# GpSimd makes two of the four weight sums of three feed-forward units

## The chip, the cores and the metric

One core of one Trainium2 chip runs the whole program in one launch. The metric is the device time of that launch in microseconds (us), as the median of several runs. All inputs start in the chip's memory, the output ends there.

## The reference, cut to what matters

Two decoder layers over 512 tokens of width 1024, in float32. The part that the change touches is the feed-forward block of each layer:

```python
h = rms_norm(x, norm_g[i, 2])
f = (jax.nn.silu(h @ w_gate[i]) * (h @ w_up[i])) @ w_down[i]
x = x + rms_norm(f, norm_g[i, 3])
```

`w_gate` and `w_up` are 1024 by 2816, `w_down` is 2816 by 1024. In front of it stand attention and a short convolution (layer 0) or a spatial gating unit (layer 1).

## The kernel before, in words

**Products.** TensorE multiplies in float32r. Each operand is split into a high part (a cast by ScalarE, `whi` or `hThi`, line 135 for weights) and a low part (operand less high part, by VectorE, `wlo` or `hTlo`, line 136), and three products of parts replace one product.

**Units.** The gate and up products of a layer run in 11 units of 256 hidden columns. In a unit the product is a two by two block product: the weights are cut into the first and the second half of the 1024 rows (chunks "a" and "b", each loaded as one `raw` tile of 128 x 2048 by two DMAs of the SyncE queue) and into two blocks of 128 columns; the 512 tokens are cut into the first and the last 256. Seven products p1 to p7 replace eight. p1, p2 and p4 use quarters of the weights as they are. The other four use sums of quarters, which VectorE makes at line 263 (tile `wsum`): s1 = a1 + b1 for p5, s2 = s1 - a0 for p6, s3 = a0 - a1 for p7, s4 = b0 - s2 for p3. Each product is 24 matmuls of line 679 (`product`), and its weights are a piece made by `Unit.piece`: `split` of a quarter or of a sum, that is one ScalarE cast and one VectorE subtraction of 128 x 1024.

**Order.** `order` is a list of pieces; `ahead` makes them some pieces before their product, and `load` starts the next `raw` chunk when fewer than three are still to be read. There are three `raw` buffers, so a chunk's load waits until the last reader of the chunk three before it has ended. `SOON` and, for the first three units, `SOON_EARLY` tell behind which piece a sum is made, ahead of its own product:

```python
        SOON = {2: ["s1"], 4: ["s3", "s2"], 6: ["s4"]}
        SOON_EARLY = {5: ["s2"], 6: ["s3"], 4: ["s4"]}
```

The three first units (`EARLY`) run p1 and p2 of the first 256 tokens while the last tokens are still being normed (`pre_norm`, `Combined.fill`), and then p5, p6, p4, p7, p3 each. The order of the instructions on VectorE, ScalarE and TensorE is made by the framework's scheduler from this program; on GpSimd it is the order of the program (`manual_schedule`).

**What else stands on GpSimd.** In the units it issues the DMAs that add up blocks of `w_down` in memory (line 186, tile `tsum`). Each stands behind a small instruction of one column, `pace` (line 779), which waits for a ScalarE or VectorE result of the unit and so keeps the DMAs in step. `power` (line 344) is another small GpSimd instruction, in the norms.

**Names.** u0 to u3 are the units of a layer in order; s3u1 is the sum s3 of u1. Line 754 (`plus`) adds a product's PSUM bank to a copy, and frees the bank; line 765 multiplies gate and up; lines 432 and 438 make the parts and sums of the tokens.

Of the kernel before, what the change touches and what calls it, by code (L numbers as in the profile page):

```python
# [72 lines left out]
def trunk(  # L73
# [6 lines left out]
    nc = tc.nc  # L80
# [11 lines left out]
    def nm(base):  # L92
        n_made[0] += 1
        return f"{base}_{n_made[0]}"
# [106 lines left out]
    class Unit:  # L201
# [4 lines left out]
        READS = {1: "a", 2: "b", 4: "b", "s1": "ab", "s2": "a", "s3": "a", "s4": "b"}  # L206
        NEEDS = {5: ["s1"], 6: ["s2"], 7: ["s3"], 3: ["s4"], "s2": ["s1"], "s4": ["s2"]}
        SOON = {2: ["s1"], 4: ["s3", "s2"], 6: ["s4"]}
        SOON_EARLY = {5: ["s2"], 6: ["s3"], 4: ["s4"]}

        def __init__(self, layer, c0):
            self.ws = [col_chunk(w[layer], c0, 256) for w in (w_gate, w_up)]
# [6 lines left out]
        def plan_first(self):  # L219
# [3 lines left out]
            self.READS = {k: v for k, v in self.READS.items() if k not in (1, 2)}  # L223
            self.SOON = self.SOON_EARLY

# [22 lines left out]
        def sum(self, s):  # L248
            if s in self.sums:
                return self.sums[s]  # L250
            for before in self.NEEDS.get(s, []):
                self.sum(before)
            t = ap_.tile([P, 2, 4, P], F32, tag="a", name=nm("wsum"))
            if s == "s1":
                x, y, op = self.quarter("a", 1), self.quarter("b", 1), ALU.add
            elif s == "s2":
                x, y, op = self.sums["s1"], self.quarter("a", 0), ALU.subtract
            elif s == "s3":
                x = self.half["a"].tile[:, :, :, 0:P]
                y, op = self.quarter("a", 1), ALU.subtract  # L260
            else:
                x, y, op = self.quarter("b", 0), self.sums["s2"], ALU.subtract
            nc.vector.tensor_tensor(out=t, in0=x, in1=y, op=op)  # L263
            self.sums[s] = t
            return t

# [40 lines left out]
    def load(upto=1000):  # L307

        while n_loaded[0] < min(upto, len(chunks)):
            if sum(c.left > 0 for c in chunks[:n_loaded[0]]) >= 3:  # L310
                return
            c = chunks[n_loaded[0]]
            c.tile = rawp.tile(c.shape, F32, tag="raw", name=nm("raw"),
                               padded_shape=[P, 2048 // math.prod(c.shape[2:])] + c.shape[2:])
            for part, view in c.views:
                if n_loaded[0] >= 2:
                    nc.sync.dma_start(out=c.tile[part], in_=view)
                else:
                    for ks in (slice(0, 2), slice(2, 4)):
                        nc.sync.dma_start(out=c.tile[:, ks, :], in_=view[:, ks, :])  # L320
            n_loaded[0] += 1
# [506 lines left out]
    with tc.manual_schedule(engines={mybir.EngineType.Activation, mybir.EngineType.DVE}):  # L828
# [37 lines left out]
        for i in range(2):  # L866
            nc.vector.tensor_tensor_reduce(
                out=lam_p, in0=lam_in[:, 2 * i, :], in1=lam_in[:, 2 * i + 1, :], scale=1.0, scalar=0.0,
# [22 lines left out]
        for i in range(2):  # L891
            nc.sync.dma_start(
                out=bias[i],
# [135 lines left out]
    for ch in range(4):  # L1029
# [8 lines left out]
        y = tmp()  # L1038
        nc.scalar.mul(out=y, in_=z[:, 2:514], mul=cols[:, 8 + ch:9 + ch])
        for i in (1, 0):  # L1040
# [8 lines left out]
                                op=ALU.subtract)  # L1049
# [144 lines left out]
```

## Time and profile before

| what | value |
|---|---|
| three runs | 1069.45, 1069.95, 1069.6 us; median 1069.6 |
| the profiled execution's own time | 1071.0 us |
| its span | 1069.1 us |
| TensorE (PE) busy | 1034.5 us, 97% of the span |
| VectorE (DVE) busy | 812.6 us, 76% |
| ScalarE (ACT) busy | 552.1 us, 52% |
| GpSimd (POOL) busy | 191.4 us, 18% |

A row of the timeline is: start in us, length in us, engine, line, operation, written tile <- read tiles, shapes, count, and in brackets the engine's idle time just before and what ended it. A row of the windows is: the stretch, its length, then busy time and number of instructions of PE, PEld (weight loads), DVE, ACT and POOL, then the granted clock of TensorE as a share of full speed, the busy share of the DMA engines and what they moved. Layer 0's units begin at about 233 us, layer 1's at about 722 us.

### The profile page before, as it was taken

The numbers are of one execution on the slowest core, as the hardware profiler recorded it, in microseconds if no ns is written. First come the engines' busy times: TensorE is split into PE (matmuls) and PEld (weight loads), VectorE is DVE, ScalarE is ACT, GpSimd is POOL, SyncE is SP. The second block draws the span as 40 slices with busy tenths as digits, with TensorE's granted clock in tenths as the row PEclk, the third lists the DMA queues.
The fourth block names the chain that finished last, engine by engine and source line by source line (L and its number), as shares of the span: only waits on it lengthen the run. The fifth ranks groups of instructions, "written<-read, shape, count | busy, mean of one in ns | idle before, by whom it ended". The sixth has DMA issues, their size and how long they took to land.

```text
span 1069.1 us, 16311 instructions
## 1 busy us (share of the span) xinstructions
PE 1034.5 (97%) x6395; PEld 923.1 (86%) x6395; DVE 812.6 (76%) x1179; ACT 552.1 (52%) x903; POOL 191.4 (18%) x259
## 2 busy tenths in 40 slices
PE   7999999998999999999999999998899999999997
PEld 5777778887899999998888788888899999998885
DVE  4466654489887996899978454679898797799974
ACT  4456453366453553584846433356455454474842
POOL 1012220011233333220000000010334343220000
PEclk7999999999999999999999999999999999999999
DMA  9231304326788798574744522414789799774741
GB/s 324 57 119 40 119 13 169 94 81 190 191 266 220 188 279 229 159 219 144 280 148 153 163 79 79 138 51 147 207 226 273 201 273 240 177 217 148 257 175 40
DMA packets 112526, 181.10 MB, mean 169 GB/s; under 512 B 5009, under 2 KB 77854, under 8 KB 110402
## 3 DMA queue, kind: packets, MB, share of 16 engines
q1 hardware_dynamic: 96578, 133.92, 38.0%
q0 software_dynamic: 15872, 46.14, 18.7%
q8 instruction: 50, 0.82, 0.3%
q14 instruction: 26, 0.21, 0.1%
HBM read 177.94 MB, written 48.24 MB: 212 GB/s over the span
## 4 chain that ended last, share of the span: by engine, by line
PE 72%; DVE 15%; DMA 4%; ACT 3%; issue 3%; POOL 1%; SPq 0%; DVEq 0%; POOLq 0%; ACTq 0%
PE ps L109 41%; PE ps L679 28%; DVE wlo L136 5%; DMA raw<-in_w_up_dram 3%; DVE wsum L263 3%; ACT whi L135 1%; POOL s L344 1%; DVE hTlo L432 1%; DVE h L503 1%; DVE t L754 1%; ACT j L491 1%; DVE x L552 1%; PE ps L952 1%; DMA raw<-in_w_in_even_dram 1%; DVE t L438 1%
## 5 line engine op out<-in xcount | busy, mean ns | idle before, releaser
L679 PE MATMUL ps<-hThi,whi 128*128 128x256 f32 x1232 | 275.1, 285 | 8.2 <-ACT whi L135 4.9
L679 PE MATMUL ps<-hThi,wlo 128*128 128x256 f32 x1232 | 275.0, 284 | 5.1 <-DVE wlo L136 5.1
L679 PE MATMUL ps<-hTlo,whi 128*128 128x256 f32 x1232 | 274.0, 284 | 1.3 <-DVE hTlo L432 1.3
L136 DVE TENSOR_TENSOR wlo<-raw,whi 128x1024 fp32r<-128x1024 f32 (+1 forms) x206 | 239.7, 1185 | 31.7 <-ACT whi L135 30.7
L135 ACT CAST whi<-raw 128x1024 fp32r<-128x1024 f32 (+1 forms) x206 | 203.6, 1018 | 27.3 <-DMA raw<-in_w_up_dram 7.8
L679 PEld LDWEIGHTS ps<-hThi,whi 128*128 128x128 f32 x1232 | 203.6, 192 | 10.6 <-ACT whi L135 5.9
L679 PEld LDWEIGHTS ps<-hThi,wlo 128*128 128x128 f32 x1232 | 204.0, 192 | 6.6 <-DVE wlo L136 6.5
L679 PEld LDWEIGHTS ps<-hTlo,whi 128*128 128x128 f32 x1232 | 203.8, 192 | 1.9 <-DVE hTlo L432 1.9
L135 ACT CAST whi<-wsum 128x1024 fp32r<-128x1024 f32 x88 | 90.1, 1045 | 57.7 <-DVE wsum L263 50.4
L109 PE MATMUL ps<-whi,wlo 128*128 128x512 f32 x308 | 119.9, 389 | 0.0
L109 PE MATMUL ps<-wlo,whi 128*128 128x512 f32 x308 | 119.8, 389 | 0.0
L109 PE MATMUL ps<-whi,whi 128*128 128x512 f32 x308 | 119.5, 390 | 0.2 <-DVE t L719 0.2
L779 POOL TENSOR_SCALAR pace<-t 128x1 f32<-128x1 f32 x96 | 74.2, 773 | 245.9 <-ACT t L764 172.4
L136 DVE TENSOR_TENSOR wlo<-wsum,whi 128x1024 fp32r<-128x1024 f32 x88 | 105.5, 1219 | 15.9 <-ACT whi L135 15.9
L344 POOL TENSOR_TENSOR s<-s,neg_half 128x1 f32<-128x1 f32 (+1 forms) x40 | 25.0, 627 | 486.8 <-DVE s L484 415.2
L754 DVE TENSOR_TENSOR t<-ps,t 128x512 f32<-128x512 f32 x88 | 58.4, 684 | 32.8 <-ACT t L759 17.6
L759 ACT COPY t<-ps 128x512 f32<-128x512 f32 x66 | 38.5, 583 | 86.2 <-PE ps L679 86.2
L109 PE MATMUL ps<-whi,a 128*128 128x512 f32 x256 | 79.9, 391 | 0.0
L186 POOL DMA_DIRECT2D tsum<-in_w_down_dram x72 | 68.4, 953 | 2.1 <-issue 0.8
L109 PEld LDWEIGHTS ps<-whi,whi 128*128 128x128 f32 x308 | 57.8, 188 | 12.6 <-issue 0.8
L109 PEld LDWEIGHTS ps<-wlo,whi 128*128 128x128 f32 x308 | 57.8, 188 | 11.9
L109 PEld LDWEIGHTS ps<-whi,wlo 128*128 128x128 f32 x308 | 57.8, 188 | 11.9
(143 smaller groups left out, 1485.8 us busy)
## 6 DMA issues: line engine op xcount, KB each, us to landing
tsum<-in_w_down_dram POOLq DMA_DIRECT2D x60, 512.0 KB, 7.0
raw<-in_w_gate_dram SPq DMA_DIRECT2D x44, 512.0 KB, 5.8
raw<-in_w_up_dram SPq DMA_DIRECT2D x44, 512.0 KB, 7.4
raw<-tsum SPq DMA_DIRECT2D x16, 1024.0 KB, 5.0
raw<-in_w_down_dram SPq DMA_DIRECT2D x12, 1024.0 KB, 5.9
raw<-in_w_in_even_dram SPq DMA_DIRECT2D x10, 1024.0 KB, 6.7
tsum<-tsum POOLq DMA_DIRECT2D x20, 512.0 KB, 5.9
raw<-in_w_in_odd_dram SPq DMA_DIRECT2D x8, 1024.0 KB, 5.4
```

Of the source, the lines that this page charges most:

```text
L109: nc.tensor.matmul(out, lhsT, rhs, start=start, stop=stop, **kw)
L135: nc.scalar.copy(out=hi, in_=src)
L136: nc.vector.tensor_tensor(out=lo, in0=src, in1=hi.bitcast(F32), op=ALU.subtract)
L186: return [lambda to=to, of=of, g=g, op=op: nc.gpsimd.dma_start(out=to[:, g, :], in_=of[:, g, :], accum_op=op) for g in self.PAIRS for op, ...
L263: nc.vector.tensor_tensor(out=t, in0=x, in1=y, op=op)
L344: nc.gpsimd.tensor_tensor(out=y0[:, :n], in0=a, in1=neg_half[:, :n], op=ALU.pow)
L432: nc.vector.tensor_tensor(out=self.part(1, p, t), in0=src, in1=self.part(0, p, t).bitcast(F32), op=ALU.subtract)
L438: minus = lambda out, x, y: nc.vector.tensor_tensor(out=out, in0=x, in1=y, op=ALU.subtract)
L679: nc.tensor.matmul(bank[:, m * 256:(m + 1) * 256], piece[a][:, m, k, :], hT.at(b, p)[:, k, :], start=first and m == 0 and i == 0, stop=i = ...
L754: nc.vector.tensor_tensor(out=c, in0=x, in1=y, op=ALU.add)
L759: nc.scalar.copy(out=c, in_=x)
L779: nc.gpsimd.tensor_scalar(out=pace, in0=at[:, 0:1], scalar1=1.0, scalar2=None, op0=ALU.mult)
```

## The change

GpSimd makes s3 and s4 of u0, u1 and u2, in both layers: 12 sums. In those units s3 is now made behind p5's piece, ahead of s2, and s4 behind p6's piece. All other units are as they were.

```diff
-        SOON_EARLY = {5: ["s2"], 6: ["s3"], 4: ["s4"]}
+        SOON_EARLY = {5: ["s3", "s2"], 6: ["s4"]}
...
-            nc.vector.tensor_tensor(out=t, in0=x, in1=y, op=op)
+            helper = self.SOON is self.SOON_EARLY and s in ("s3", "s4")
+            engine = nc.gpsimd if helper else nc.vector
+            engine.tensor_tensor(out=t, in0=x, in1=y, op=op)
```

Lines behind it move down by two. On GpSimd, at the start of layer 0's units, before (`raw_2205` and `raw_2255` are chunks a and b of u0, `raw_2331` is a of u1):

```order
L344 TENSOR_TENSOR s_2241<-s_2239,neg_half 128x1
L779 TENSOR_SCALAR pace_2198<-t_2468 128x1
L779 TENSOR_SCALAR pace_2198<-t_2509 128x1
L186 DMA tsum_77<-in_w_down_dram 128x2x512
L779 TENSOR_SCALAR pace_2198<-t_2575 128x1
```

and now:

```order
L346 TENSOR_TENSOR s_2241<-s_2239,neg_half 128x1
L265 TENSOR_TENSOR wsum_2376<-raw_2205 128x1024
L265 TENSOR_TENSOR wsum_2437<-raw_2255,wsum_2378 128x1024
L781 TENSOR_SCALAR pace_2198<-t_2470 128x1
L781 TENSOR_SCALAR pace_2198<-t_2509 128x1
L186 DMA tsum_77<-in_w_down_dram 128x2x512
L265 TENSOR_TENSOR wsum_2583<-raw_2331 128x1024
L781 TENSOR_SCALAR pace_2198<-t_2575 128x1
```

s3u0 and s4u0 stand ahead of all the paced DMAs, s3u1 behind the second `pace` and its DMA.

On VectorE, at the turn from u2 to u3, before (`raw_2662` and `raw_2798` are a and b of u3, whose sums stay on VectorE; the two instructions of line 754 free the banks of u2's last products):

```order
L136 TENSOR_TENSOR wlo_2967<-raw_2798,whi_2966 128x1024
L263 TENSOR_TENSOR wsum_2970<-raw_2662,raw_2798 128x1024
L136 TENSOR_TENSOR wlo_3007<-raw_2798,whi_3006 128x1024
L754 TENSOR_TENSOR t_2998<-ps_2875,t_2996 128x512
L754 TENSOR_TENSOR t_3002<-ps_2874,t_2996 128x512
L765 TENSOR_TENSOR a_2649<-t_2998 128x256
L263 TENSOR_TENSOR wsum_3010<-raw_2662 128x1024
```

and now:

```order
L136 TENSOR_TENSOR wlo_2967<-raw_2768,whi_2966 128x1024
L265 TENSOR_TENSOR wsum_2970<-raw_2662,raw_2768 128x1024
L136 TENSOR_TENSOR wlo_3007<-raw_2768,whi_3006 128x1024
L265 TENSOR_TENSOR wsum_3010<-raw_2662 128x1024
L265 TENSOR_TENSOR wsum_3012<-wsum_2970,raw_2662 128x1024
L756 TENSOR_TENSOR t_2998<-ps_2875,t_2996 128x512
L756 TENSOR_TENSOR t_3002<-ps_2874,t_2996 128x512
```

Two sums of u3 have come ahead of the two instructions that free the banks. The orders of TensorE and of the SyncE queue are almost as before.

## Rows read from the trace of the kernel before

**Rows 1.** Windows, columns as told above: layer 0's units and the slow clock.

```profile
250.00:265.00 15.00, 12.43 (x98) 11.62 (x97) 15.00 (x21) 8.00 (x12) 2.34 (x1) 1.00 0.48 144
...
304.00:308.00 4.00, 2.21 (x13) 2.01 (x12) 4.00 (x7) 0.84 (x2) 0.91 (x2) 0.83 0.36 137
308.00:312.00 4.00, 4.00 (x28) 4.00 (x27) 2.20 (x4) 1.12 (x2) 0.66 (x1) 0.75 0.66 172
312.00:316.00 4.00, 4.00 (x36) 4.00 (x35) 4.00 (x5) 3.67 (x5) 2.64 (x4) 1.00 0.98 275
```

**Rows 2.** Timeline of PE, layer 0: matmuls that waited.

```profile
256.51 0.38 PE L679 MATMUL ps<-hThi,whi 128*128 128x256 f32 x1 [1.83 <-ACT whi L135]
...
267.23 0.38 PE L679 MATMUL ps<-hThi,wlo 128*128 128x256 f32 x1 [0.88 <-DVE wlo L136]
...
271.84 0.39 PE L679 MATMUL ps<-hThi,wlo 128*128 128x256 f32 x1 [0.88 <-DVE wlo L136]
...
287.39 0.38 PE L679 MATMUL ps<-hThi,wlo 128*128 128x256 f32 x1 [0.88 <-DVE wlo L136]
...
306.46 0.47 PE L679 MATMUL ps<-hThi,whi 128*128 128x256 f32 x1 [1.79 <-DVE t L754]
```

**Rows 3.** Timeline of PE, layer 1: matmuls that waited.

```profile
749.98 0.74 PE L679 MATMUL ps<-hTlo,whi 128*128 128x256 f32 x4 [0.81 <-DVE hTlo L432]
...
761.33 0.74 PE L679 MATMUL ps<-hThi,wlo 128*128 128x256 f32 x4 [0.52 <-DVE wlo L136]
...
777.35 0.74 PE L679 MATMUL ps<-hThi,wlo 128*128 128x256 f32 x4 [0.52 <-DVE wlo L136]
...
795.22 0.74 PE L679 MATMUL ps<-hThi,whi 128*128 128x256 f32 x4 [0.57 <-DVE t L754]
```

**Rows 4.** Timeline of DVE, layer 0: the queue around the sums.

```profile
246.22 0.68 DVE L432 TENSOR_TENSOR hTlo<-t,hThi 128x512 fp32r<-128x512 f32 x1
...
254.17 1.22 DVE L263 TENSOR_TENSOR wsum<-wsum,raw 128x1024 f32<-128x1024 f32 x1
...
257.98 1.22 DVE L263 TENSOR_TENSOR wsum<-raw 128x1024 f32<-128x1024 f32 x1
...
262.05 1.22 DVE L263 TENSOR_TENSOR wsum<-raw,wsum 128x1024 f32<-128x1024 f32 x1
...
268.22 1.22 DVE L263 TENSOR_TENSOR wsum<-raw,raw 128x1024 f32<-128x1024 f32 x1
...
305.13 1.28 DVE L754 TENSOR_TENSOR t<-ps,t 128x512 f32<-128x512 f32 x2
```

**Rows 5.** Chain that ended last: start us, us, what; loads of u2's b and u3's b.

```profile
276.83 6.82 DMA raw<-in_w_up_dram
...
292.38 8.17 DMA raw<-in_w_up_dram
```

**Rows 6.** Timeline of POOL: instructions beside VectorE's, and the second pace.

```profile
96.54 0.93 POOL L933 TENSOR_SCALAR t<-t,s 128x256 f32<-128x256 f32 x1
...
261.02 2.34 POOL L779 TENSOR_SCALAR pace<-t 128x1 f32<-128x1 f32 x1 [19.16 <-ACT t L759]
265.73 0.38 POOL L779 TENSOR_SCALAR pace<-t 128x1 f32<-128x1 f32 x1 [2.37 <-ACT t L764]
...
619.48 1.10 POOL L1115 TENSOR_SCALAR_AFFINE_SELECT a<-a 128x1024 f32<-128x1024 f32 x1
```

**Rows 7.** Timeline of DVE at two of these places.

```profile
96.67 1.43 DVE L136 TENSOR_TENSOR wlo<-raw,whi 128x1024 fp32r<-128x1024 f32 x1
...
619.55 1.04 DVE L350 TENSOR_TENSOR s<-s 128x1 f32<-128x1 f32 x1 [0.66 <-POOL s L344]
```

**Rows 8.** Groups of instructions by line and form: names, count | busy us, mean ns.

```profile
L136 DVE TENSOR_TENSOR wlo<-raw,whi 128x1024 fp32r<-128x1024 f32 x192 | 230.6, 1221 | 31.7 <-ACT whi L135 30.7 <-PE ps L109 0.3
...
L350 DVE TENSOR_TENSOR s<-s 128x1 f32<-128x1 f32 x36 | 6.6, 183 | 11.9 <-POOL s L344 11.2
...
L933 POOL TENSOR_SCALAR t<-t,s 128x512 f32<-128x512 f32 x4 | 6.3, 1566 | 20.1 <-PE ps L918 6.3 <-ACT t L1033 4.9 <-DVE t L1036 4.9
...
L933 POOL TENSOR_SCALAR t<-t,s 128x128 f32<-128x128 f32 x4 | 2.4, 609 | 37.3 <-DVE s L932 33.1 <-ACT a L1010 4.2
```

## The prediction, made before the changed kernel was run

> **What bounds the kernel now.** I read the windows first, to find where TensorE is not full. In layer 0's units, from 250 to 265 us, TensorE is busy 12.43 of 15 us while VectorE is busy all 15 [rows 1]. So VectorE is the bound of that stretch. The PE timeline then says what each stop waits for: a high or low part of a weight sum in u0 and u1 (1.83, 0.88 and 0.88 us), the low part of s1u2 (0.88), and at 306.46 a bank that VectorE frees late (1.79) [rows 2]. Behind that last stop the granted clock falls to 0.83 and 0.75, and 28 matmuls run in 4 us where 36 run afterwards [rows 1]: 8 x 4/36 = 0.9 us lost there and some 0.6 us ahead of it, 1.5 us in all. Layer 1 has the same stops, smaller at the end (0.81, 0.52, 0.52, 0.57) [rows 3]. Once the units run steadily TensorE does not stop, so what the starts gain or lose passes to the end. Nearly all that can be won is in these stops.
>
> **How VectorE and GpSimd meet.** Most of VectorE's instructions here read two tensors from SBUF (wlo, the sums, hTlo<-t,hThi); those with a PSUM operand read one. The trace shows the two engines holding each other up. The one-column `pace` at 261.02 took 2.34 us, the next one 0.38 [rows 6]: it ended only when a row of VectorE instructions with two SBUF operands ended. The other way round: at 619.48 GpSimd begins an instruction that reads 1024 elements and takes 1.10 us, and a one-column VectorE instruction with two SBUF operands, begun 0.07 us later, takes 1.04 us, to the very end of it [rows 6, 7], against a mean of 0.18 [rows 8]. With a GpSimd instruction of 256 elements (96.54, 0.93 us) a wlo begun 0.13 us later took 1.43 us instead of 1.22 [rows 6 to 8]: held by 0.2 us, not to the end. So GpSimd's reading holds VectorE's two-operand instructions, and the hold goes with what is read.
>
> **The change part by part.**
>
> *Price of one sum on GpSimd.* No GpSimd tensor_tensor of this size is in the trace. The hold, T, lies between 1.0 us (the 619.48 row, if both operands were read at once) and the whole instruction at line 933's pace: (1566 - 609)/384 = 2.5 ns an element [rows 8], 0.61 + 896 x 2.5 ns = 2.85 us. I take 2.1 us, twice 1.04, since two operands of 1024 are read and the 619.48 row is the nearest in size.
>
> The Trainium skill (SBUF — State Buffer, Who interferes with whom) has the shared port pair held for the whole instruction, and the loser fully blocked. The 96.67 row does not bear this out: by it wlo would have ended at 97.47 + 1.22 and not at 98.10. The Trainium skill (GPSIMD Engine Reference, Performance versus the Vector engine) gives 4497 ns for a float32 tensor_tensor of 2048 elements; half of it, my estimate, is 2.25 us, and with T at that the sum below would be some 0.6 us longer in each layer.
>
> *Saved on VectorE.* Each sum's slot is 1.13 us, from its start to the next start (257.98, 262.05) [rows 4]. So a sum on GpSimd costs VectorE 2.1 - 1.13 = 1 us, unless it falls beside instructions with a PSUM operand or an idle VectorE.
>
> *Layer 0, u0.* s3u0 needs only chunk a, which is there at about 246.3, and stands first in GpSimd's queue. VectorE runs hTlo until 246.90 [rows 4]; GpSimd gets in at its end and holds to 249.0, where the next instruction would have begun at 246.83: +2.15. Nothing has been saved yet, so s1 and s2, and TensorE's stops for p5 and p6, are later by that. s4u0 needs s2 (254.17 + 2.15, 1.22 long), and gets in behind the instruction then running: +2.1. Only then come the two empty slots: -2.27. s1u1 (268.22) is later by 2.15 + 2.1 - 2.27 = 2.0. The wait for wlo of s3u0 at 267.23 vanishes in TensorE's own lateness.
>
> *u1.* s3u1 stands behind the second `pace` (265.73) [rows 6] and its DMA, whose instruction takes about 0.8 us; with +2.0 it asks at about 268.9, and holds wlo of s4u0 or s1u1: +2.1. The low part for p5u1 (271.84) comes 4.1 us later, and TensorE with it. s4u1 stands behind s2u1, beside two instructions of line 754 with PSUM operands, 1.2 of its 2.1 us covered: +0.9. The two slots give -2.27, and about 1.1 us in which VectorE stood idle in u1 are used up. s1u2 is +4.1 + 0.9 - 2.27 - 1.1 = 1.6 later; s3u2 in front of it adds 2.1: 3.7. TensorE's wait of 0.88 at 287.39 shrinks a little: +3.7 there.
>
> *Loads.* Chunk b of u2 now needs no s3 on VectorE, which released its buffer at about 276.4 (its DMA runs from 276.83) [rows 5]; but s2u1, now 4.1 later, ends at about 277, so this load gains nothing. The same holds for u3's b (292.38, 8.17 us): its release moves by +0.3.
>
> *u2 to u3.* VectorE frees the banks (305.13, two of line 754) behind two more sums than before, 2.27 us: they end at 306.41 + 0.3 + 2.27 = 309.0. TensorE is there at 304.67 + 3.7, less 0.5 for four matmuls that now follow: 307.9. It waits 1.1 instead of 1.79 us and goes on 2.5 later. If the clock holds, 1.5 us come back: +1.0 for layer 0. I take that it holds: the stops of 0.88 us cost no clock, nor did that of 1.83 (granted clock 1.00 in 250 to 265).
>
> *Layer 1.* The same queue, +4.1 at 761.33; s1u2's waits shrink by about 0.4, the stop of 0.57 at 795.22 goes, no clock to win: +3.2.
>
> *At nothing.* The paced DMAs issue up to 3 us later; their sums are read in the down product, over 100 us on. GpSimd's 12 sums are some 30 us of an engine that is 18% busy.
>
> The sum: +1.0 + 3.2 = +4.2 us. The profiled execution took 1071.0 us (span 1069.1, 1.9 around it), 1.4 over the median; against it the sum is 1075.2, and from the median, which the runs are compared by, 1069.6 + 4.2 = **1073.8 us**. About 0.2%, 2.1 us, can be told from no change.
>
> **The rivals.**
>
> *VectorE keeps its turn (faster).* GpSimd may get in only where VectorE reads PSUM or idles; the `pace` at 261.02 passed two ends of VectorE instructions before it got in, which speaks for it; other `pace` rows got in at the first end. Then s3u0 costs 2.1 - 0.6 = 1.5, s4u0 lies beside three PSUM instructions (263.19 to 264.99): 0.3; less 2.27, s1u1 is 0.5 earlier; s3u1 in VectorE's idle 1.1 us behind s1u1 adds 1.0: +0.5. The stop at 287.39 goes (-0.88), that at 306.46 shrinks and the clock holds: -2.5 in layer 0, -1.2 in layer 1. 1065.9 us. It decides where a sum's uncovered hold falls under 1.13 us.
>
> *No hold at all for a two-operand read (faster).* Then VectorE gains 2.27 us before s1u1, s3 ends early, the loads of b come some 5 us earlier, and the stops at 287.39 and 306.46 go with the slow clock: 2.27 + 0.88 + 1.79 + 1.5 = 6.4 in layer 0, 2.27 + 1.1 + 0.57 = 3.9 in layer 1: 1059.3 us. The rows at 96.67 and 619.55 speak against it.
>
> *The hold is the whole instruction at line 933's pace.* T = 2.85, three holds in a row on the path of each layer: 0.75 x 3 x 2 = 4.5 more: 1078.3 us.
>
> **How the numbers follow.** The forecast 0.5 (its own range 1070 to 1077.5), VectorE keeping its turn 0.2, no hold 0.15, the long hold 0.15. The range 1064 to 1079 leaves out the case of no hold and the ends of the others, 0.2 in all. Faster by over 0.2% (under 1067.5): 0.15 + 0.14 + 0.02 = 0.31. Within it: 0.06 + 0.13 = 0.19. Slower: 0.35 + 0.15 = 0.50.
>
> **What would show it.** Right: GpSimd sums of some 2 us or more; at the end of each, a VectorE instruction with two SBUF operands that began early and lasted up to 2 us too long; p5u0's low part some 2 us later, p5u1's 4; no clock below 1.00 around 306; TensorE's stop there near 1 us. Wrong: VectorE instructions of normal length beside the sums; GpSimd sums of 4 us and more that stretch until VectorE reads PSUM (the first rival); loads of u2's b issued several us earlier than 276.4, with p5u2 not later than 287.4.

## The result and the profile after

The changed kernel takes 1084.2 us in the median (1083.3 to 1087.0) beside 1069.8 of the kernel before: a ratio of 1.0135, 95% interval 1.0118 to 1.0153, so 14.5 us slower. The sign was forecast, at half a chance; the size was not: 1073.8 us, with a range that ended at 1079. Two executions of the kernel `fill` (1696 and 3588 us) and one of `s2_then_s3` (1135 us) fell in a slow state of the chip and stand in no figure below.

The page of the changed kernel, busy time by engine (the table of before has 1034.5, 812.6, 552.1 and 191.4 us):

```profile
PE 1038.2 (96%) x6395; PEld 926.8 (86%) x6395; DVE 822.8 (76%) x1167; ACT 551.3 (51%) x903; POOL 227.8 (21%) x271
```

VectorE has lost twelve sums of 1.22 us, 14.6 us of work, and is busy 10 us longer than before: the time in which it is held counts as busy. Groups of the changed kernel by line and form (names, count | busy us, mean ns), the two forms of sum on GpSimd and VectorE's `wlo` of sums:

```profile
L265 POOL TENSOR_TENSOR wsum<-raw 128x1024 f32<-128x1024 f32 x6 | 16.5, 2758 | 4.5 <-DMA raw<-in_w_up_dram 4.5
L265 POOL TENSOR_TENSOR wsum<-raw,wsum 128x1024 f32<-128x1024 f32 x6 | 15.0, 2496 | 35.7 <-DVE wsum L265 27.1 <-issue 8.6
...
L136 DVE TENSOR_TENSOR wlo<-wsum,whi 128x1024 fp32r<-128x1024 f32 x88 | 121.5, 1399 | 17.6 <-ACT whi L135 17.6
```

Before, these 88 `wlo` took 105.5 us, 1219 ns each; they alone have grown by 16 us.

Where it happens is seen by laying two timelines side by side. Timeline of GpSimd after, layer 0: s3u0, s4u0, s3u1 with the DMA ahead of it, s4u1, and s3u2 with its DMA:

```profile
245.35 3.51 POOL L265 TENSOR_TENSOR wsum<-raw 128x1024 f32<-128x1024 f32 x1 [4.15 <-DMA raw<-in_w_up_dram]
256.49 2.67 POOL L265 TENSOR_TENSOR wsum<-raw,wsum 128x1024 f32<-128x1024 f32 x1 [7.63 <-DVE wsum L265]
...
269.55 0.80 POOL L186 DMA_DIRECT2D tsum<-in_w_down_dram  x1
270.37 2.44 POOL L265 TENSOR_TENSOR wsum<-raw 128x1024 f32<-128x1024 f32 x1
...
278.59 2.38 POOL L265 TENSOR_TENSOR wsum<-raw,wsum 128x1024 f32<-128x1024 f32 x1 [3.92 <-DVE wsum L265]
...
286.33 1.24 POOL L186 DMA_DIRECT2D tsum<-in_w_down_dram  x1
287.12 2.91 POOL L265 TENSOR_TENSOR wsum<-raw 128x1024 f32<-128x1024 f32 x1
```

Timeline of VectorE after, the instructions beside them:

```profile
245.56 0.68 DVE L434 TENSOR_TENSOR hTlo<-t,hThi 128x512 fp32r<-128x512 f32 x1
246.16 0.42 DVE L767 TENSOR_TENSOR a<-t 128x256 f32<-128x256 f32 x1
246.50 0.68 DVE L440 TENSOR_TENSOR t<-ps,a 128x512 f32<-128x512 f32 x1
247.10 2.85 DVE L136 TENSOR_TENSOR wlo<-raw,whi 128x1024 fp32r<-128x1024 f32 x1
...
256.87 2.57 DVE L767 TENSOR_TENSOR a<-t 128x256 f32<-128x256 f32 x1
...
268.99 0.42 DVE L767 TENSOR_TENSOR a<-t 128x256 f32<-128x256 f32 x1 [2.47 <-ACT t L766]
269.33 4.56 DVE L136 TENSOR_TENSOR wlo<-wsum,whi 128x1024 fp32r<-128x1024 f32 x2
273.82 1.21 DVE L265 TENSOR_TENSOR wsum<-raw,raw 128x1024 f32<-128x1024 f32 x1
276.14 1.23 DVE L136 TENSOR_TENSOR wlo<-wsum,whi 128x1024 fp32r<-128x1024 f32 x1 [1.11 <-ACT whi L135]
...
278.42 1.28 DVE L756 TENSOR_TENSOR t<-ps,t 128x512 f32<-128x512 f32 x2
279.61 2.44 DVE L136 TENSOR_TENSOR wlo<-wsum,whi 128x1024 fp32r<-128x1024 f32 x1
...
286.71 5.54 DVE L136 TENSOR_TENSOR wlo<-wsum,whi 128x1024 fp32r<-128x1024 f32 x2 [0.52 <-ACT whi L135]
```

Read them in pairs. s4u0 ends at 256.49 + 2.67 = 259.16; the product `a` begun at 256.87 ends at 259.44, 2.15 us longer than its usual 0.42. s4u1 ends at 280.97; the `wlo` begun at 279.61 ends at 282.05, 1.08 us behind it, as if it had only begun there. At 247.10 too `wlo` ends 1.09 us behind the end of s3u0 (248.86). So a VectorE instruction with two SBUF operands makes no progress until GpSimd's sum has ended. Those that read PSUM are untouched: `t<-ps,a` at 246.50 lasts 0.68, as the same instruction did before (at 247.16), and the two of line 756 at 278.42 take 1.28, as they do alone [rows 4].

When a sum gets in differs. s4u0 and s3u1 did so at the first end of a VectorE instruction. s3u0 did not: it was issued at 245.35, passed the ends of `hTlo` and `a`, and ended 2.36 us behind 246.50, where VectorE turned to PSUM; undisturbed a sum takes 2.35 us (s3u0 of layer 1, at 740.04).

And TensorE. Timeline of PE after, layer 0:

```profile
254.01 0.39 PE L681 MATMUL ps<-hThi,whi 128*128 128x256 f32 x1 [0.71 <-ACT whi L135]
255.27 0.39 PE L681 MATMUL ps<-hThi,wlo 128*128 128x256 f32 x1 [0.87 <-DVE wlo L136]
257.48 0.39 PE L681 MATMUL ps<-hThi,whi 128*128 128x256 f32 x1 [1.83 <-ACT whi L135]
260.11 0.58 PE L681 MATMUL ps<-hTlo,whi 128*128 128x256 f32 x1 [2.24 <-DVE hTlo L434]
...
276.16 0.38 PE L681 MATMUL ps<-hThi,whi 128*128 128x256 f32 x1 [2.44 <-ACT whi L135]
277.42 0.38 PE L681 MATMUL ps<-hThi,wlo 128*128 128x256 f32 x1 [0.88 <-DVE wlo L136]
...
295.78 0.38 PE L681 MATMUL ps<-hThi,wlo 128*128 128x256 f32 x1 [0.88 <-DVE wlo L136]
...
313.57 0.39 PE L681 MATMUL ps<-hThi,whi 128*128 128x256 f32 x1 [0.80 <-DVE t L756]
```

Windows after, columns as in rows 1:

```profile
254.00:258.00 4.00, 1.16 (x3) 0.56 (x3) 4.00 (x5) 2.41 (x4) 1.51 (x1) 1.00 0.22 55
258.00:262.00 4.00, 1.90 (x9) 1.90 (x10) 4.00 (x5) 1.53 (x4) 1.16 (x1) 0.54 0.74 248
262.00:266.00 4.00, 4.00 (x24) 4.00 (x23) 4.00 (x7) 2.49 (x4) 0.61 (x1) 0.61 0.23 65
...
278.00:282.00 4.00, 4.00 (x24) 4.00 (x23) 4.00 (x5) 2.61 (x4) 3.41 (x2) 0.60 0.58 161
...
744.00:752.00 8.00, 8.00 (x60) 8.00 (x59) 8.00 (x13) 3.52 (x6) 0.00 (x0) 0.85 0.42 133
...
756.00:760.00 4.00, 3.10 (x14) 3.10 (x15) 4.00 (x6) 1.52 (x4) 0.19 (x1) 0.58 0.48 163
```

The four stops up to 260.11 add to 5.65 us; TensorE worked 1.16 us of the 4 from 254 on, and then ran at the lower of its two levels (1.2 GHz) for most of 258 to 266. A second fall follows the stops of 2.44 and 0.88 us at p5u1. Layer 1 has two falls as well, but the first stands behind a stop of 3.64 us for `h` at 743.44 (1.55 before) and the second behind p6u0's stops; behind p5u1's stops of 2.47 and 0.52 us its clock stays at 1.00. In 4 us TensorE does 36 of these matmuls at full clock [rows 1], so the windows at 258, 262 and 278 lost 0.9 + 1.3 + 1.3 us, those of layer 1 1.3 + 1.5 us.

How late TensorE is at each point, against the kernel before, is worked out from the same matmul in both profiles. The change entered layer 0's units 0.67 us earlier (a matmul at 252.97 before is at 252.30) and layer 1's 6.13 us later (723.65 and 729.78); that is taken off.

| TensorE later by (us) | forecast | layer 0 | layer 1 |
|---|---|---|---|
| p5u0, low part; in layer 1 the stop for `h` ahead of u0 | 2.15 | 255.27 - 254.30 + 0.67 = 1.6 | 743.44 - 735.22 - 6.13 = 2.1 |
| p5u1, low part | 4.1 | 277.42 - 271.84 + 0.67 = 6.3 | 772.35 - 761.33 - 6.13 = 4.9 |
| p5u2, low part | 3.7 | 295.78 - 287.39 + 0.67 = 9.1 | 790.01 - 777.35 - 6.13 = 6.5 |
| bank at the turn to u3 | 2.5 | 313.57 - 306.46 + 0.67 = 7.8 | 807.76 - 795.22 - 6.13 = 6.4 |
| behind the turn | +1.0 and +3.2 | 6.8 | 6.9 |

The sum of the last line, 13.7, less the 0.67, is the 13.2 us between the two profiled spans (1082.3 and 1069.1), to 0.2 us. Between the two layers nothing is added: TensorE is 6.8 us late at 318 us and at 723 us.

### The profile page after: what moved, and what is told of

It reads as the page before. It is cut to its first block, busy times and chain, and to the rows that moved or that the text cites. A ratio compares the mean times of both kernels' runs of the same rounds, so it can differ in the third digit from the quotient of the medians.

```text
span 1082.3 us, 16319 instructions
## 1 busy us (share of the span) xinstructions
PE 1038.2 (96%) x6395; PEld 926.8 (86%) x6395; DVE 822.8 (76%) x1167; ACT 551.3 (51%) x903; POOL 227.8 (21%) x271
## 4 chain that ended last, share of the span: by engine, by line
PE 72%; DVE 17%; ACT 4%; issue 3%; DMA 2%; POOL 1%; SPq 0%; DVEq 0%; POOLq 0%; ACTq 0%
PE ps L109 39%; PE ps L681 29%; DVE wlo L136 6%; DVE wsum L265 3%; DMA raw<-in_w_up_dram 1%; POOL s L346 1%; ACT whi L135 1%; DVE t L756 1%; DVE h L505 1%; ACT j L493 1%; DVE hTlo L434 1%; DVE a L767 1%; DVE x L554 1%; PE ps L954 1%; DMA raw<-in_w_in_even_dram 1%
## 5 line engine op out<-in xcount | busy, mean ns | idle before, releaser
L136 DVE TENSOR_TENSOR wlo<-wsum,whi 128x1024 fp32r<-128x1024 f32 x88 | 121.5, 1399 | 17.6 <-ACT whi L135 17.6
L781 POOL TENSOR_SCALAR pace<-t 128x1 f32<-128x1 f32 x96 | 80.5, 839 | 171.9 <-ACT t L766 140.6
L766 ACT ACTIVATE t<-t 128x256 f32<-128x256 f32 x88 | 36.3, 417 | 62.7 <-DVE t L756 62.6
```

Source lines behind the costliest of these rows:

```text
L136: nc.vector.tensor_tensor(out=lo, in0=src, in1=hi.bitcast(F32), op=ALU.subtract)
L766: nc.scalar.activation(out=c[:, 0:256], in_=c[:, 0:256], func=AF.Silu)
L781: nc.gpsimd.tensor_scalar(out=pace, in0=at[:, 0:1], scalar1=1.0, scalar2=None, op0=ALU.mult)
```

## The experiments

Ratios are those to the kernel before on the same chip, with their 95% intervals; times are medians.

**The order or GpSimd.** The first two kernels part the change in its two halves.

```diff
-            helper = self.SOON is self.SOON_EARLY and s in ("s3", "s4")
+            helper = False
```

> The new order of the sums, with all of them on VectorE. Theory of the hold (the loss comes from GpSimd's sums, each of which stops VectorE's two-operand instructions for about 2.2 us in place of a slot of 1.13): this kernel loses nothing of the 14.6 us; 1068 to 1071 us (s2u0 and with it p6u0 1.1 later, but u2's chunk b loaded 1 to 2 us earlier, so that the stop of 0.88 before p5u2 shrinks). Rival, the order (s2 behind s3, and two more sums of u3 ahead of the instructions that free the banks): at least half of the loss, 1077 us or more.

Measured: 1068.2 us, 0.9987 (0.9975 to 0.9999). The order alone loses nothing and may even gain 0.1%.

```diff
-        SOON_EARLY = {5: ["s3", "s2"], 6: ["s4"]}
+        SOON_EARLY = {5: ["s2"], 6: ["s3"], 4: ["s4"]}
```

(in the changed kernel, the sums still on GpSimd)

> The old order of the sums, with s3 and s4 of u0 to u2 on GpSimd. Theory of the hold: nearly all of the loss, 1081 to 1087 us, since the sums still come in at the same data. Rival, the order: 1070 to 1074 us.

Measured: 1081.6 us, 1.0101 (1.0074 to 1.0128). GpSimd's sums cost most of the loss in either order. Timeline of PE with the new order and all sums on VectorE, and two windows of it:

```profile
258.29 0.38 PE L681 MATMUL ps<-hThi,whi 128*128 128x256 f32 x1 [2.96 <-ACT whi L135]
...
288.93 0.39 PE L681 MATMUL ps<-hThi,wlo 128*128 128x256 f32 x1 [0.54 <-DVE wlo L136]
```

```profile
258.00:262.00 4.00, 3.63 (x19) 3.43 (x20) 4.00 (x6) 2.55 (x5) 0.00 (x0) 0.69 0.79 266
262.00:266.00 4.00, 4.00 (x32) 4.00 (x32) 4.00 (x7) 2.29 (x5) 1.21 (x1) 0.88 0.37 112
```

s2u0 is 1.13 later, as expected, and makes the stop for p6u0 2.96 instead of 1.83; in return the stop of 0.88 before p5u2 is down to 0.54, and the stop of 1.79 at the turn to u3 [rows 2] is gone (its window, 304 to 308, has 35 matmuls at a granted clock of 1.00 where rows 1 have 13 at 0.83). The clock falls here too, behind the one stop of 2.96, but at little price: counted as in the table above (this kernel entered the units 0.64 us later), TensorE is 2.0 us late there (260.45 before, 263.10 here) and 0.7 us at p5u1 (270.58 and 271.89).

**Which sums.** The changed kernel with GpSimd making the sums of fewer units (`number` is the unit's place in its layer), or s4 alone:

```diff
-            helper = self.SOON is self.SOON_EARLY and s in ("s3", "s4")
+            helper = self.number == 0 and s in ("s3", "s4")
```

> New order; GpSimd makes s3 and s4 of u0 alone. Theory of the hold with the clock: VectorE's queue is full there, so both holds pass to TensorE (1.6 and 1.8 us), TensorE's clock falls behind these stops and costs some 2 us more, and some of it is taken up by the stops that follow: +3 to +4 us in each layer, 1076 us (1074 to 1079). Rival, only the holds count and the clock is an onlooker: 2.2 + 2.2 - 2.3 = 2 us in each layer, 1074 us or less. Rival, the sums of u1 and u2 are the loss: 1071 us or less.

Measured: 1073.7 us, 1.0031 (1.0020 to 1.0043): just under the range that the first theory gave, just inside that of its rival without the clock; it does not part them.

```diff
+            helper = self.number in (1, 2) and s in ("s3", "s4")
```

> New order; GpSimd makes s3 and s4 of u1 and u2, those of u0 stay on VectorE. Theory of the hold: s3u1 (2.2 us) and s3u2 (3.2 us with the paced DMA) stand ahead of the first sums of u1 and u2 and pass to TensorE; s4 lies half beside instructions that read PSUM and costs what its slot saves; 2 to 2.5 us come back at the turn to u3 in layer 0: 1075 us (1073 to 1078), and with u0_only it adds up to the change's 14.6 us within 2. Rival, u0's late TensorE is what makes the later sums costly (VectorE idle behind it): u12_only within 2 us of before, 1068 to 1072.

Measured: 1078.0 us, 1.0071 (1.0047 to 1.0095). u1 and u2 are costly with u0 untouched, so the rival that puts it on u0 falls.

```diff
+            helper = self.SOON is self.SOON_EARLY and s == "s4"
```

> New order; GpSimd makes s4 of u0 to u2 alone, s3 is VectorE's. Theory of the hold by place: s4u0 falls among instructions with two SBUF operands (2.2 us, less the slot of 1.13, and the clock), s4u1 and s4u2 lie half beside instructions that read PSUM and cost about what their slot saves: 1069.5 to 1072.5 us, so that s3 makes up most of the loss. Rival, every sum on GpSimd costs the same: half of the 16 us between order_only and the change, 1075 to 1077.

Measured: 1075.3 us, 1.0054 (1.0038 to 1.0070). Missed: the expectation took s4u0 at too little. The time is even in the range of its rival, that every sum costs the same; the next kernel parts the two. Timeline of PE with s4 alone on GpSimd:

```profile
257.02 0.39 PE L681 MATMUL ps<-hThi,whi 128*128 128x256 f32 x1 [2.96 <-ACT whi L135]
259.64 0.58 PE L681 MATMUL ps<-hTlo,whi 128*128 128x256 f32 x1 [2.23 <-DVE hTlo L434]
```

Two stops of 2.96 and 2.23 us, 2.6 us apart: s4u0 brings the second, and the clock is 0.50 from 258 to 262.

```diff
+            helper = self.number in (1, 2) and s == "s4"
```

> New order; GpSimd makes s4 of u1 and u2 alone (four sums), where two instructions that read PSUM stand behind s2 on VectorE. Theory of the hold by place: 1.2 of the 2.2 us of hold are covered, the slot saves 1.13: within 1 us of order_only, 1067.5 to 1069.5 us. Rival, every sum on GpSimd costs the same: 16 us/12 each, 1073 to 1074 us.

Measured: 1070.0 us, 1.0007 (0.9996 to 1.0019), 0.5 us over its range and far from the rival. In its timeline s4u1 (274.65, 2.40 us) lies beside the two PSUM instructions, and the `wlo` behind them takes 2.51: held for 1.3 us, beside a saved slot of 1.13.

Against the order alone (0.9987) the ratios rise by 0.44% for all of u0, 0.84% for u1 and u2, 1.48% for the whole: 4.7, 9.0 and 15.8 us, nearly additive. s4 of u1 and u2 is 0.20%, 2.1 us for four sums; s4u0 is 0.54 - 0.07 = 0.47%, 5.0 us for two; so s3u0 has no price beside the order alone (4.7 - 5.0), and s3 of u1 and u2 has 9.0 - 2.1 = 6.9 us for four. The differences are good to some 2 us each, so that the parts show where the price is high, not how high to a microsecond.

**What is held, and for how long.** In the kernel with u1 and u2 alone, GpSimd's instruction reads one operand:

```diff
+            if helper:
+                nc.gpsimd.tensor_scalar(out=t, in0=x, scalar1=1.0, scalar2=None, op0=ALU.mult)
```

> As u12_only, but GpSimd's eight instructions read one operand (a copy with a scale of 1; the other operand of s3 and s4 of u1 and u2 is left out, so the sums are not made). Theory, the hold goes with what GpSimd reads (0.85 to 1.1 us for 1024 elements, as at 96.67 and 619.48 in the trace of before): VectorE's instructions beside them are 1 us too long instead of 2.2, 1070 to 1073 us. Rival, GpSimd holds VectorE for the whole instruction whatever it reads: at line 933's pace 2.5 to 2.85 us each, 1077 us or more.

Measured: 1072.3 us, 1.0025 (1.0012 to 1.0038), where the two-operand form had 1078.0. Timeline of GpSimd, then of VectorE, in this kernel:

```profile
265.54 2.83 POOL L266 TENSOR_SCALAR wsum<-raw 128x1024 f32<-128x1024 f32 x1
...
269.64 2.79 POOL L266 TENSOR_SCALAR wsum<-raw 128x1024 f32<-128x1024 f32 x1
```

```profile
264.49 3.19 DVE L136 TENSOR_TENSOR wlo<-wsum,whi 128x1024 fp32r<-128x1024 f32 x2
...
269.93 1.85 DVE L136 TENSOR_TENSOR wlo<-wsum,whi 128x1024 fp32r<-128x1024 f32 x1 [1.11 <-ACT whi L135]
```

GpSimd's instruction is longer than a sum, and yet the two `wlo` at 264.49 are 3.19 - 2.35 = 0.84 us too long, and the one at 269.93 ends at 271.78 while GpSimd works until 272.43. (The kernel leaves out an operand, so its result is not the program's.) One operand of 1024 elements holds VectorE for 0.84 us of 2.83; two hold it to the end, 2.2 us.

**The price of the clock.** The changed kernel with matmuls that TensorE does where it stood still. The first try put 20 into a free bank:

> The changed kernel with 20 further matmuls in u0 of each layer (into a bank that is still free, their result is overwritten), placed where TensorE would stop for p6u0 and for the low parts of the tokens. Theory: TensorE's clock falls there because TensorE stood idle, and costs about 2.2 us in layer 0 (258 to 266 us at 0.54 and 0.61) and 1.4 us in layer 1: with the stops filled the clock stays at 1.00 and 2 to 4 us come back, 1080 to 1082.5 us. Rival, the slow clock hides behind VectorE's lateness anyway: 1084 us or, by the added matmuls, up to 1087.

Measured: 1083.5 and 1084.5 us. No trace of these two executions shows whether the matmuls fell into the stops and the clock held, so it decides nothing. The second:

```diff
+                if m == 0 and i == (1 if by_k else 7):
+                    for _ in range(fill):
+                        nc.tensor.matmul(bank[:, 0:256], zeros, hT.at(0, 1)[:, 0, :],
+                                         start=False, stop=False, skip_group_check=True)
...
-                run(q, u, 5)
+                run(q, u, 5, fill=(32, 18)[layer] if i == 0 else 0)
```

> The changed kernel with matmuls of zero weights (32 in layer 0, 18 in layer 1; they add nothing to p5's bank) between the first matmuls of p5u0 and those that wait for the low parts of the tokens, so that TensorE is busy from 255.4 to about 259.7 us instead of standing for 4 us. Theory: the clock fell behind these stops (0.54 and 0.61 from 258 to 266 us) and costs time of its own, because p6u0's end releases the ScalarE copy, the silu and the product a for which VectorE waited 2.5 us at 268.99: 258 to 266 us at 0.9 or more, p5u1 2 us earlier, 1080 to 1082 us in all. Rival: the end is set by VectorE's holds, and the slow clock lies beside them: 1083 to 1085 us at whatever clock.

Measured: 1082.9 us, 1.0130 (1.0113 to 1.0146). That lies just above the theory's range and just under its rival's, and 0.05% under the change's ratio; the time alone does not part them. Windows of this kernel:

```profile
254.00:258.00 4.00, 2.42 (x18) 2.02 (x17) 4.00 (x6) 2.13 (x4) 0.15 (x1) 1.00 0.49 172
258.00:262.00 4.00, 3.25 (x28) 3.05 (x27) 4.00 (x4) 2.72 (x4) 2.59 (x1) 1.00 0.74 234
262.00:266.00 4.00, 4.00 (x36) 4.00 (x35) 4.00 (x6) 2.06 (x3) 0.61 (x1) 1.00 0.10 33
...
768.00:772.00 4.00, 3.77 (x18) 3.47 (x19) 4.00 (x5) 2.06 (x5) 1.56 (x1) 0.57 0.39 111
```

In the first three the clock stays at 1.00, and the wait of 2.47 us at 268.99 on VectorE is gone (`a` follows at 267.87 without a gap). Timeline of PE:

```profile
275.03 0.39 PE L683 MATMUL ps<-hThi,whi 128*128 128x256 f32 x1 [1.97 <-ACT whi L135]
```

This kernel entered the units 0.70 us later than the one before, so p5u1's first matmul (270.58 there) is 3.75 us late here, and in the change 276.16 - 270.58 + 0.67 = 6.25: the first fall of the clock costs 2.5 us in layer 0, and the same 2.5 us are still there behind the turn to u3 (6.8 and 4.3 us late at 318). In layer 1 the clock stays at 1.00 from 752 to 760 too, but only 0.4 us come back (6.5 us late behind the turn, not 6.9). Two things differ there: VectorE waits only 0.57 us for ScalarE behind p6u0 in the change (at 763.89), so there is less to win, and in this kernel the clock falls behind p5u1 (0.57 from 768 to 772), where the change had 1.00. Since the two medians came from different chips, the change and this kernel were then run on one:

> The changed kernel itself, as the yardstick for fill2_again and fill3 on the same chip: 1084 us (1083 to 1086), 1.35% over the kernel before.

> fill2 once more, beside the change on the same chip. Theory, the slow clock behind u0's stops has a price: 1.5 to 3 us under change_again. Rival, the clock only fills time in which TensorE would wait for VectorE: within 0.7 us of it.

Measured: 1086.1 us, 1.0154 (1.0133 to 1.0176), and 1082.4 us, 1.0121 (1.0103 to 1.0140): 3.7 us apart, somewhat more than expected, on intervals that overlap a little. The two profiled executions differ by more (spans of 1086.6 and 1078.3 us), and 3.6 us of that arise between 321 and 686 us, away from the units' starts; at p5u1 it is 6.3 and 3.75 us again, and behind the turn 6.8 and 4.25, so 2.5 us in layer 0 is the better figure. A third kernel added 20 matmuls ahead of p5u1:

> fill2 with 20 more matmuls of zero weights ahead of p5u1, where TensorE stops for 2.4 us in both layers and the clock then falls to 0.60 (278 to 282 us). Theory: the clock stays at 1.00 there too and another 1 to 1.5 us a layer come back: 3 to 6 us under change_again, 1078.5 to 1081 us. Rival: VectorE sets p5u2, so nothing more comes back: within 0.7 us of fill2_again, or above it by the added matmuls.

Measured: 1087.7 us, 1.0169 (1.0148 to 1.0190). It tells nothing of the clock: the added matmuls moved `wlo` and `a` on VectorE in u1 and u2, and two stops of 1.58 and 1.83 us stand at 297.60 and 299.94 that the change does not have; the stop that they were to fill stayed, at 3.10 us. What the second fall costs in layer 0 was not settled. For layer 1 the change's own two executions give a figure. Windows of the first, then of the second, behind p5u1's stops (2.47 and 0.52 us, 2.45 and 0.28 us):

```profile
772.00:776.00 4.00, 3.65 (x30) 3.65 (x31) 4.00 (x5) 2.54 (x4) 2.42 (x2) 1.00 0.32 77
```

```profile
772.00:776.00 4.00, 1.27 (x6) 0.96 (x6) 2.89 (x4) 1.53 (x2) 0.98 (x2) 0.85 0.49 131
776.00:780.00 4.00, 4.00 (x26) 4.00 (x27) 4.00 (x4) 2.62 (x4) 3.05 (x2) 0.73 0.44 127
```

From p5u1 to p5u2 TensorE takes 17.66 us in the first (772.35 to 790.01) and 18.00 in the second (775.73 to 793.73): the fall costs 0.3 us, and VectorE waits 0.26 us for TensorE in between (at 782.50), in the first not at all. So nearly the same stops came with a fall in one execution and without in the other.

**A better order.** Two more orders with all sums on VectorE:

```diff
-        SOON_EARLY = {5: ["s2"], 6: ["s3"], 4: ["s4"]}
+        SOON_EARLY = {5: ["s2", "s3"], 6: ["s4"]}
```

> All sums on VectorE, with s3 of the early units right behind s2 (not ahead of it) and s4 behind p6's piece. If order_only gains because s3 ends earlier and frees its chunk (u2's b loaded earlier, the bank at the turn to u3 not late), and loses 1.1 us at p6 of u0 because s2 waits for s3, then this keeps the gain without the loss: 1066 to 1068 us, TensorE's stop for p6u0 back at 1.8 us from 2.96. If the gain of order_only came from somewhere else, 1068.5 us or more.

Measured: 1073.7 us, 1.0034 (1.0021 to 1.0046). Missed on the wrong side. Its timeline of PE:

```profile
276.31 0.39 PE L679 MATMUL ps<-hThi,wlo 128*128 128x256 f32 x1 [0.86 <-DVE wlo L136]
...
294.06 0.39 PE L679 MATMUL ps<-hThi,wlo 128*128 128x256 f32 x1 [0.88 <-DVE wlo L136]
```

With s3 right behind s2, the `wlo` of s2 comes a slot later while its `whi` does not, and TensorE stops for p6's low part in u1 and u2, where the kernel before has no stop.

```diff
+            self.SOON = self.SOON_EARLY if self.number == 0 else self.SOON_NEXT
...
+        SOON_NEXT = {5: ["s3", "s2"], 6: ["s4"]}
```

> All sums on VectorE; u0 in the old order (s2 at once, since TensorE waits for it there), u1 and u2 in the new one (s3 ahead of s2, so that their chunks are freed early). Theory: the loss of order_only at p6u0 (a stop of 2.96 instead of 1.83, and the clock behind it) goes, its gain in u1 and u2 stays: 1066 to 1067.8 us. Rival: the gain comes with u0's order, 1068.5 to 1070 us.

Measured: 1068.1 us, 0.9988 (0.9979 to 0.9997). TensorE's stop at p6u0 is back at 1.83 and its turn to u3 free, as expected; the clock stays at 1.00 from 250 to 270, where the new order throughout had 0.69 and 0.88. The time is no better than with that order, 0.3 us over the range. It is, with that one, the fastest here: 0.1% under the kernel before, and all on VectorE.

## Why the prediction was wrong in size

**The hold was right; its price came out partly by luck.** T was taken as 2.1 us, twice what one operand was read to have cost at 619.48 [rows 6, 7]; measured are 2.15 to 2.2 us where nothing covers it, and 0.84 for one operand. The row at 619.55 says the same if the instruction's own 0.18 us are taken off its 1.04: 0.86. Twice that is 1.7; two operands hold VectorE not twice as long as one but for the whole sum, which happens to last 2.35 to 2.44 us. The row of 0.2 us for 256 elements at 96.67 fits one operand: 256 x 0.83 ns. The Trainium skill (SBUF — State Buffer, Who interferes with whom) has the loser blocked for the whole instruction; with two operands that agrees (ends 1.08 us behind the sum's), with one it does not (0.84 of 2.83 us), and the measurement decides. The three rivals fall as they were priced. VectorE did not keep its turn at s4u0, which got in at the first end of a VectorE instruction (256.95), between two with SBUF operands, nor at s3u1; at s3u0 of layer 0 it did, and there the price is the rival's (1.6 us, 1.5 forecast by it). What decides it was not tried. The hold is there. The third rival was right that with two operands the hold is the whole instruction, but the instruction is not 2.85 us long.

**The steps up to p5u1 hold at full clock.** The forecast had TensorE 4.1 us late there. With the clock kept up (fill2) it is 3.75 in layer 0 and, worked out likewise, 4.2 in layer 1. The parts are less right than the sum: s3u0 cost 1.6, not 2.15, since 0.6 us of it lay beside `t<-ps,a`, and against the order alone, where its slot on VectorE delays p6u0, it has no price at all.

**The step that failed first: the clock behind u0's stops, which stands at nothing in the sum.** The forecast weighed the clock only at the turn to u3 ("I take that it holds", which came true there: 1.00 from 306 on), from single stops of 0.88 and 1.83 us that cost none. For the stops of u0, which it made longer by two holds, it had no term. They came to 5.65 us in 7. The clock fell, the matmuls behind p6u0 began 5.3 us late (3.25 in fill2), and that came back to VectorE: ScalarE's copy of p6u0 stands ahead of the silu that `a` needs, and `a` ahead of s1u1. So VectorE waited 2.47 us at 268.99, where the forecast had it full. Timeline of ACT after:

```profile
268.05 0.59 ACT L761 COPY t<-ps 128x512 f32<-128x512 f32 x1 [2.68 <-PE ps L681]
268.54 0.42 ACT L766 ACTIVATE t<-t 128x256 f32<-128x256 f32 x1
```

So p5u1 is 6.3 late instead of 4.1. That is 2.5 of the 5.8 us by which layer 0 missed. At the turn to u3 the forecast was nearly right: 1.2 us were to be won by a shorter wait and 1.5 by the clock, and 1.3 (9.1 to 7.8) and 1.0 (7.8 to 6.8) were. The forecast shows no working for VectorE's +0.3 there; measured it came from 9.1 to 7.8 - 2.27 = 5.5, so that the 3.4 us which that term takes off were about right (3.6).

**The second, and in both layers together the larger: u1, "about 1.1 us in which VectorE stood idle in u1 are used up", and 2.1 for s3u2.** From s1u1 to s1u2 VectorE took 283.76 - 268.22 = 15.54 us before and 292.18 - 273.82 = 18.36 now: 2.8 more, where the forecast had 0.4 less. The idle of 1.11 us is still there at 276.14: it is the wait for ScalarE's cast of the sum just made, and moves with the sum. All idle in this stretch grew from 2.2 to 2.8 us. And the two `wlo` at 286.71 took 5.54 instead of 2.35: s3u2 held for 3.2 us, not 2.1. So 4.4 us of holds (1.2 for s4u1), less 2.27 saved, plus 0.6 of idle, give the 2.8: 3.2 us more than forecast, and in layer 1, where TensorE's lateness grows by 1.6 from p5u1 to p5u2, 2.0 more.

**The third: what the stops take up.** The forecast let the stop of 0.88 before p5u2 shrink; it is 0.88 at 295.78, and 0.52 in layer 1 as before, since both ends of it wait for the same late sum.

**Layer 1** has the same errors but lacks the turn to u3, where layer 0 wins 2.3 us back (9.1 to 6.8). Its s3u0 did not fall beside `wlo` but into the last norm ahead of the units: p5u1 is 4.9 late (4.1 forecast), p5u2 6.5 (3.7). The stop of 0.57 us at the turn, which was to go, is 0.77.

Of what was to show the forecast right, the sums, the VectorE instructions that last 2 us too long and TensorE's stop near 1 us at 306 (0.80) came; "no clock below 1.00" was said only of 306, and was not looked for where the new stops stand. The loads of u2's chunk b were issued at 278.56 (276.42 before): no gain there, as forecast.

## What to carry to other kernels

Work handed to an engine that holds up the one to be relieved is no relief by itself: compare the hold on the old engine (2.2 us) with the slot that it saves (1.13), and look for places where the old engine reads PSUM, since those instructions kept their length (the four sums that lay half beside such cost 2.1 us in all; none lay wholly beside them). Where TensorE already stops for VectorE, add up the stops that a change sets close together before taking the clock as given, and ask who waits for the slowed matmuls: the fall cost 2.5 us in layer 0, where VectorE waited 2.47 for them, and 0.3 us behind p5u1 of layer 1, where it waited 0.26. And an idle stretch is a cushion only if it does not wait for the very thing that is late.

## What the runs showed beyond that

- A GpSimd instruction with one operand held VectorE for 0.83 ns an element in the sizes seen (0.84 us of 2.83 for 1024, 0.2 for 256), one with two for its whole length.
- Where GpSimd's sum follows a DMA instruction whose row has not yet ended (the DMA at 286.33 lasts to 287.57, the sum begins at 287.12), VectorE was held 1 us longer: 3.2 instead of 2.2 with two operands, 1.84 instead of 0.84 with one. There the first of the two `wlo` at 286.71 was held too, though it began 0.41 us ahead of the sum's row: it took 4.41 us. But it is not so everywhere: in the kernel with one operand the instruction at 286.15 follows a DMA that lasts to 286.56, and VectorE's sum at 285.25 is held for 0.84 us only. Why was not tried.
- Three new orders of the same sums on VectorE lie between 1068.1 and 1073.7 us, with single slots of 1.13 us moved.
